# A hybrid sequence layer on one core: gates computed in three parts, decay rows stored from GpSimd's queue, and first-phase stores issued by the engine that made the data

## The chip, the cores and the metric

The kernel runs on one core of a Trainium2 chip. The metric is the device time of one execution in microseconds; the profile shows what each engine did in one such execution. The engines are TensorE (PE; its weight loads are listed as PEld), VectorE (DVE), ScalarE (ACT), GpSimd (POOL) and SyncE (SP), which here only issues DMAs.

## The reference

One layer for two groups: a prompt of 1024 frames and 32 sample frames that continue running streams, all of width 1024. The input is normalised and modulated by adaLN. One combined projection feeds three head groups: four mLSTM heads (a matrix memory), eight heads of forgetting attention (FoX) and a gated MLP. What they give is joined, goes through one output projection and a layer norm, then through a SwiGLU feed-forward layer and a second layer norm. Keys, values, log-forget rows and the mLSTM's final state are outputs too. The part that the change reorders is the gates: for FoX the running sum of the log-forget values enters each score,

```
Ft = jnp.cumsum(logf, axis=1).transpose(0, 2, 1)
logits = (jnp.einsum('bthd,bshd->bhts', qi, k) * FOX_SCALE
          + Fi[..., None] - Ft[:, :, None, :])
```

and for the mLSTM a running maximum over input gate minus forget sum gives the stabiliser `m`, block by block.

## The kernel before

Every matrix product is made from high and low parts in a reduced fp32 format (three products instead of one: L117 to L119 with weights stationary, L282 to L284 with tokens stationary). Weights come by DMA, ScalarE casts the high part (L105), and VectorE or GpSimd makes the low part (L106).

The first phase (`run`) computes for the 1088 columns of the prompt and the samples: first units of the projection (`fm_first`), the FoX values and the gate columns (`tm_unit` with `evac_v`, which fills the tile `G`), then `gates()`, and then a list of units written out in the string `ORDER`. Its letters: `q0` to `q7` are the heads' query and key projections (`head_unit`: products `head_g` for the first 512 columns, `fm_g` for more), `f0` to `f7` the attention of the first four query tiles of a head (`fox`: scores `fox_s`, probabilities `fox_p`, their transposes `fox_t`, outputs `fox_o`), `k` the mLSTM's queries and keys (`fm_unit` with `evac_mqk`), `s` the mLSTM states, `m0` to `m3` mLSTM blocks, `v` and `o` the mLSTM's values and output gates (`evac_raw`), and `a` one unit of the adaLN projection (`ada`, weights in `ada_late`, products at L179, result copied at L182). After the list come the gated MLP, the second halves of the later heads, the output projection, layer norm 1 and the feed-forward part.

The framework's scheduler turns this into one queue of instructions for each engine, from its own estimate of times; attention and mLSTM are put under a higher priority. Within an engine instructions run in queue order, and a wait at the head of a queue holds everything behind it. DMAs issued from SP and from ScalarE also wait until the earlier transfer that used the same one of eight completion counters has landed.

`gates()` takes `G`, makes the log-sigmoid on VectorE, sums along frames with matrix products (L484 to L487), joins the sums of the eight blocks (L497), and writes the decay rows: a tile `fr` of 64 x 6 x 128 with the running sums and their negatives in high and low parts and with ones, stored to the DRAM tile `dfs` by two DMAs. The heads read them back with `decay()` into the last four partitions of `q2` and `k2` (tiles `head_q`, `head_k`), and L769, the second of the two products of a score, needs them; L768, the first, does not. Then `gates()` makes the running maxima by seven VectorE steps, a recurrence over nine blocks (L525 and the lines around), with products at L521 and L529, and the column form of the weights for the mLSTM (`col`, transposed at L547). Its last stores are the states `o_m` and `o_ms` and the tiles `dM` and `dd0` in DRAM. Its tiles lie in a pool of their own that is closed at its end.

All stores of the first phase are issued from SP, in one queue with all loads. GpSimd issues DMAs only late in the kernel (`start_dp`, from 927.6 us on).

Of the kernel before, what the change touches and what calls it, by code (L numbers as in the profile page):

```python
# [15 lines left out]
P = 128  # L16
# [4 lines left out]
NS = 32  # L21
# [48 lines left out]
class Kernel:  # L70
# [18 lines left out]

    def store(self, out, in_):  # L90
        self.nc.sync.dma_start(out, in_)

# [207 lines left out]
    def evac_v(self, half):  # L300
        nc = self.nc

        def evac(tt, ps, n):
            nc.vector.tensor_copy(self.G[:n, tt, 8 * half:8 * half + 8], ps[:n, 256:264])
            cols = slice(256 * half, 256 * half + 256)
            if tt == 8:
                nc.vector.tensor_copy(self.vs[:, cols], ps[:n, :256])
                self.store(self.d["o_vs"][:, cols], self.vs[:, cols])
                return
            raw = self.t(self.sm, [P, 256], F32, "traw", 2)  # L310
            nc.scalar.copy(raw, ps[:, :256])
            self.store(self.d["o_v"][tt * P:(tt + 1) * P, cols], raw)
            hl = self.t(self.sm, [P, 4, 2, 64], F32R, "vhl", 2)
            src = ps[:, :256].rearrange("p (h e) -> p h e", h=4)
            nc.vector.tensor_copy(hl[:, :, 0, :], src)
            nc.vector.tensor_tensor(hl[:, :, 1, :], src, f(hl[:, :, 0, :]), ALU.subtract)
            self.store(self.dv[:, tt, 512 * half:512 * half + 512],
                       f(hl).rearrange("p h two e -> p (h two e)"))
        return evac

    def evac_raw(self, dst):
        nc = self.nc

        def evac(tt, ps, n):
            if tt < 8:
                raw = self.t(self.sm, [P, 256], F32, "traw", 2)
                nc.scalar.copy(raw, ps[:, :256])
                self.store(dst[:, tt, :], raw)
            else:
                self.store(dst[:n, tt, :], ps[:n, :256])  # L330
        return evac
# [27 lines left out]
    def evac_qk(self, h):  # L359
        nc = self.nc  # L360

        def evac(o, n, ps):
# [5 lines left out]
            nc.gpsimd.tensor_tensor(kr[:, :n], f(hi[:, :n]), f(lo[:, :n]), ALU.add)  # L368
            self.store(self.dqh[h, :, o:o + n], f(hi[:, :n]))
            self.store(self.dql[h, :, o:o + n], f(lo[:, :n]))  # L370
            self.store(self.d["o_kT"][h, :, o:o + n], kr[64:, :n])
            if o + n == T:
# [14 lines left out]
    def head_unit(self, h):  # L387
# [17 lines left out]
        for o in (0, 256):  # L405
            kr = self.t(self.sm, [P, 272], F32, "qkr", 2)
            nc.scalar.copy(kr[hi, :256], ps[hi, o:o + 256])
            self.store(self.d["o_kT"][h, :, o:o + 256], kr[hi, :256])
        self.store(self.dqh[h, hi, :512], f(k1[hi]))
        self.store(self.dql[h, hi, :512], f(k2[lo]))  # L410
# [8 lines left out]
    def evac_mqk(self, i, scale):  # L419
        nc = self.nc  # L420

        def evac(o, n, ps):
            r = self.t(self.sm, [P, 272], F32, "qkr", 2)
            nc.scalar.activation(r[:, :n], ps, AF.Copy, scale=scale)
            self.store(self.dmqk[:, i, o:o + n], r[:, :n])
        return evac


    def gates(self):
        self.phase = "gates"  # L430
        nc, d = self.nc, self.d
        ctx = ExitStack()
# [3 lines left out]
        ut = t([64, 64], "ut")  # L436
        nc.gpsimd.memset(ut[:, 0:8], 0.0)
# [3 lines left out]
        rows = self.ident[:R, :R].rearrange("p (j h) -> p j h", h=4)  # L441
        ind, sel, back = t([R, 9], "ind"), t([R, 4], "sel"), t([4, R], "back")
        nc.vector.tensor_reduce(ind, rows, AX.X, ALU.add)
# [3 lines left out]
        pair = lambda x: x.unsqueeze(1).to_broadcast([R, 2, 9])  # L447
        scan = [t([R, 192], "scan0"), t([R, 192], "scan1")]
        for x in scan:
            nc.gpsimd.memset(x[:, 0:64], NEG)  # L450
        fr = t([64, 6, P], "fr", F32R)
        nc.gpsimd.memset(f(fr[:, 2:4, :]), 1.0)
        m0 = t([4, 9], "m0")
        nc.vector.memset(m0[:, 0:1], NEG)
        mm = t([4, 2, 9], "mm")
        self.load(mm[:, 0, 8:9], d["state_m"])

        x = t([P, 9, 16], "gx")
        nc.vector.tensor_tensor(x, self.G, self.rowp[:, 0:16].unsqueeze(1).to_broadcast([P, 9, 16]), ALU.add)
        z = x[:, :, 4:16]  # L460
        a, e, s, s2, p = (t([P, 9, 12], f"g{i}") for i in range(5))
        nc.vector.scalar_tensor_tensor(a, z, -1.0, z, ALU.mult, ALU.min)
# [9 lines left out]
        nc.vector.tensor_scalar(a, z, 0.0, None, ALU.min)  # L472
        ls = t([P, 9, 12], "ls")
# [3 lines left out]
        gi, gm, gn, gf = (t([P, 9, n], f"gw{i}") for i, n in enumerate((4, 4, 4, 8)))  # L477
        nc.vector.tensor_copy(gf, ls[:, :, 4:12])
# [9 lines left out]

        rf = t([72, P], "rf")
        nc.scalar.copy(rf, ps[:72, 256:384])  # L490
        nc.vector.tensor_copy(scan[0][:, 64:192], ps[:R, 0:128])
        rs = t([R, 4, P], "rs")
        nc.scalar.copy(rs[:, 0, :], ps[:R, 0:128])
        b = t([R, P], "gb")
# [3 lines left out]
        fc = t([64, 1], "fc")  # L498
        nc.vector.tensor_copy(fc, pc[:64, 0:1])
        ft = t([64, P], "ft")  # L500
        nc.vector.tensor_scalar(ft, rf[:64], fc, None, ALU.add)
        nc.scalar.copy(fr[:, 4, :], ft)
        nc.vector.tensor_tensor(fr[:, 5, :], ft, f(fr[:, 4, :]), ALU.subtract)
        nc.vector.tensor_scalar(fr[:, 0:2, :], f(fr[:, 4:6, :]), -1.0, None, ALU.mult)
        for r in (slice(0, 32), slice(32, 64)):
            self.store(self.dfs[r], f(fr[r]))
        nc.vector.tensor_copy(self.sf[64:72, :], rf[64:72, 0:NS])

        for i in range(7):
# [3 lines left out]
        A = scan[1][:, 64:]  # L513
        E = t([R, 2], "E")
# [4 lines left out]
        EI = t([R, 2, 9], "EI")  # L519
        nc.vector.tensor_tensor(EI, E.unsqueeze(2).to_broadcast([R, 2, 9]), pair(ind), ALU.mult)  # L520
        nc.tensor.matmul(pc[:4, 32:50], sel, EI.rearrange("p a j -> p (a j)"), start=True, stop=True)  # L521
        ab = t([4, 2, 9], "ab")
        nc.vector.tensor_copy(ab, pc[:4, 32:50].rearrange("p (a j) -> p a j", a=2))
# [5 lines left out]
        nc.tensor.matmul(pc[:R, 64:82], back, mm.rearrange("p a j -> p (a j)"), start=True, stop=True)  # L529
        mt, mc = t([R, 2, 9], "mt"), t([R, 2], "mc")  # L530
        nc.vector.tensor_tensor(mt, pc[:R, 64:82].rearrange("p (a j) -> p a j", a=2), pair(ind), ALU.mult)
        nc.vector.tensor_reduce(mc, mt, AX.X, ALU.add)
        M = t([R, P], "M")
# [4 lines left out]
        self.store(self.dM, M)  # L538
        self.store(d["o_m"], m0[:, 8:9])
        mes, d0 = t([4, 1], "mes"), t([4, 9], "d0")  # L540
        nc.vector.tensor_tensor(mes, mm[:, 1, 8:9], ab[:, 1, 8:9], ALU.add)
        self.store(d["o_ms"], mes)
        nc.vector.tensor_tensor(d0, mm[:, 0, :], mm[:, 1, :], ALU.subtract)
        self.store(self.dd0, d0)
        ps = self.t(self.pt, [P, 512], F32, "t")
# [3 lines left out]
        nc.scalar.activation(self.col[:, :, 1:4, :], self.col[:, :, 1:4, :], AF.Exp)  # L549
        ctx.close()  # L550

# [128 lines left out]
    def to_mix(self, x, j, L, k0, pool, bank=None):  # L680
# [8 lines left out]
        o = j * P - GO[c]  # L689
        self.store(self.dmix[c][:, k0:k0 + 2, o:o + L], s[:, :, :L])  # L690


    def evac_gmlp(self, tt, ps, n, bank=None):
# [28 lines left out]
        w = n * nt  # L722
        self.store(self.dmix[c][:, 6:8, o:o + w], s.rearrange("p i t q -> p i (t q)")[:, :, :w])

# [577 lines left out]
    def run(self):  # L1302
# [343 lines left out]
```

## Time and profile before

| | |
|---|---|
| median of 3 runs | 1389.02 us (1388.13 to 1390.63) |
| profiled execution | 1390.74 us, span 1389.0 us |
| TensorE busy | 1341.3 us, 97% |
| VectorE busy | 1013.7 us, 73% |
| ScalarE busy | 653.7 us, 47% |
| GpSimd busy | 236.2 us, 17% |
| mean granted TensorE clock | 0.988 |

Busy times are sums over one execution. An engine at 97% leaves 48 us of idle time in the whole span, so single waits of one to three microseconds matter, and they are read one by one from TensorE's timeline. The granted clock is a share of full speed: at 0.50 a product takes twice as long.

### The profile page before, as it was taken

The numbers are of one execution on the slowest core, as the hardware profiler recorded it, in microseconds if no ns is written. First come the engines' busy times: TensorE is split into PE (matmuls) and PEld (weight loads), VectorE is DVE, ScalarE is ACT, GpSimd is POOL, SyncE is SP. The second block draws the span as 40 slices with busy tenths as digits, with TensorE's granted clock in tenths as the row PEclk, the third lists the DMA queues.
The fourth block names the chain that finished last, engine by engine and source line by source line (L and its number), as shares of the span: only waits on it lengthen the run. The fifth ranks groups of instructions, "written<-read, shape, count | busy, mean of one in ns | idle before, by whom it ended". The sixth has DMA issues, their size and how long they took to land.

```text
span 1389.0 us, 25227 instructions
## 1 busy us (share of the span) xinstructions
PE 1341.3 (97%) x9432; PEld 1224.2 (88%) x9432; DVE 1013.7 (73%) x2144; ACT 653.7 (47%) x1274; POOL 236.2 (17%) x269
## 2 busy tenths in 40 slices
PE   7997999999999899999999999999999999999996
PEld 4896899988899778888887889899999999999996
DVE  5546643678779757777776766677998988888777
ACT  3313444553545544545544445345574554545355
POOL 1000100032156600000000000264610000000341
PEclk9999899999999999999999999999999999999998
DMA  9764664455765665444443442564597768463321
GB/s 360 252 225 122 187 186 129 128 170 157 224 202 159 171 199 182 125 131 137 135 134 86 107 127 80 187 171 133 160 239 188 214 165 212 139 175 112 102 91 65
DMA packets 123513, 224.65 MB, mean 162 GB/s; under 512 B 21260, under 2 KB 66232, under 8 KB 123392
## 3 DMA queue, kind: packets, MB, share of 16 engines
q1 hardware_dynamic: 118080, 212.95, 49.4%
q0 software_dynamic: 5168, 9.96, 4.6%
q8 instruction: 74, 1.21, 0.4%
q14 instruction: 47, 0.39, 0.1%
q10 hardware_dynamic: 144, 0.14, 0.0%
HBM read 191.21 MB, written 51.72 MB: 175 GB/s over the span
## 4 chain that ended last, share of the span: by engine, by line
PE 83%; DVE 7%; DMA 4%; ACT 2%; issue 2%; SPq 1%; POOL 1%; DVEq 0%; ACTq 0%; POOLq 0%
PE up_g L117 5%; PE up_g L118 5%; PE up_g L119 5%; PE dn_g L119 4%; PE dn_g L117 4%; PE dn_g L118 4%; PE sup_u L119 3%; PE sup_u L117 3%; PE sup_u L118 3%; PE tm_g L283 3%; PE tm_g L282 2%; PE tm_g L284 2%; PE wo_g L119 2%; PE wo_g L117 2%; PE wo_g L118 2%; PE fox_t L804 2%
## 5 line engine op out<-in xcount | busy, mean ns | idle before, releaser
L117 PE MATMUL up_g<-mlstm_ah,up_whi 128*128 128x512 f32 (+1 forms) x384 | 142.2, 371 | 5.1 <-ACT lna_tmp L1053 3.3
L118 PE MATMUL up_g<-mlstm_al,up_whi 128*128 128x512 f32 (+1 forms) x384 | 142.2, 370 | 0.4 <-DVE mlstm_al L1058 0.4
L119 PE MATMUL up_g<-mlstm_ah,up_wlo 128*128 128x512 f32 (+1 forms) x384 | 141.3, 368 | 0.0
L283 PE MATMUL tm_g<-tm_wlo,start_h1h 128*128 128x256 f32 (+1 forms) x384 | 109.4, 286 | 0.9 <-DVE tm_wlo L106 0.9
L282 PE MATMUL tm_g<-tm_whi,start_h1h 128*128 128x256 f32 (+1 forms) x384 | 109.1, 286 | 0.3 <-DVE tm_traw L352 0.2
L284 PE MATMUL tm_g<-tm_whi,start_h1l 128*128 128x256 f32 (+1 forms) x384 | 109.1, 285 | 0.0
L1177 ACT CAST sup_whi<-sup_raw 128x1024 fp32r<-128x1024 f32 x54 | 56.0, 1048 | 91.0 <-PE dn_u L118 47.6
L117 PEld LDWEIGHTS up_g<-mlstm_ah,up_whi 128*128 128x128 f32 x384 | 73.6, 192 | 17.5 <-ACT mlstm_ah L1057 3.5
L118 PEld LDWEIGHTS up_g<-mlstm_al,up_whi 128*128 128x128 f32 x384 | 73.7, 192 | 11.9 <-DVE mlstm_al L1058 1.1
L119 PEld LDWEIGHTS up_g<-mlstm_ah,up_wlo 128*128 128x128 f32 x384 | 73.8, 192 | 10.8
L777 ACT ACTIVATE fox_p<-fox_s,fox_fmx 128x384 f32<-128x384 f32 (+2 forms) x96 | 55.2, 579 | 57.2 <-DVE fox_fmx L775 43.6
L105 ACT CAST up_whi<-up_raw 128x1024 fp32r<-128x1024 f32 x50 | 52.4, 1048 | 61.6 <-PE dn_g L118 20.9
L1032 DVE SCALAR_TENSOR_TENSOR wo_z<-dn_g,start_mod,wo_z 128x512 f32<-128x512 f32 (+4 forms) x120 | 60.2, 519 | 22.5 <-PE dn_g L119 22.0
L1178 DVE TENSOR_TENSOR sup_wlo<-sup_raw,sup_whi 128x1024 fp32r<-128x1024 f32 x54 | 68.1, 1264 | 10.8 <-ACT sup_whi L1177 10.8
L106 DVE TENSOR_TENSOR up_wlo<-up_raw,up_whi 128x1024 fp32r<-128x1024 f32 x50 | 66.8, 1336 | 12.3 <-ACT up_whi L105 11.6
L283 PEld LDWEIGHTS tm_g<-tm_wlo,start_h1h 128*128 128x128 f32 x384 | 72.2, 188 | 2.6 <-issue 1.2
L282 PEld LDWEIGHTS tm_g<-tm_whi,start_h1h 128*128 128x128 f32 x384 | 72.1, 189 | 1.8 <-DVE tm_traw L352 0.7
L117 PE MATMUL dn_g<-up_acth,dn_whi 128*128 128x512 f32 (+2 forms) x200 | 73.5, 368 | 0.0
L118 PE MATMUL dn_g<-up_actl,dn_whi 128*128 128x512 f32 (+2 forms) x200 | 73.3, 368 | 0.0
L119 PE MATMUL dn_g<-up_acth,dn_wlo 128*128 128x512 f32 (+2 forms) x200 | 73.3, 366 | 0.0
L284 PEld LDWEIGHTS tm_g<-tm_whi,start_h1l 128*128 128x128 f32 x384 | 72.2, 188 | 0.5 <-issue 0.4
L105 ACT CAST dn_whi<-dn_raw 128x1024 fp32r<-128x1024 f32 (+1 forms) x44 | 42.7, 971 | 51.0 <-PE up_g L118 11.4
(641 smaller groups left out, 4605.5 us busy)
## 6 DMA issues: line engine op xcount, KB each, us to landing
up_raw<-w_gu SPq DMA_DIRECT2D x50, 512.0 KB
dn_raw<-w_dn SPq DMA_DIRECT2D x28, 512.0 KB
ada_late<-w_ada SPq DMA_DIRECT2D x24, 512.0 KB
wo_raw<-w_o SPq DMA_DIRECT2D x24, 512.0 KB
sup_raw<-w_gu SPq DMA_DIRECT2D x20, 512.0 KB
start_dp<-w_gu SPq DMA_DIRECT2D x19, 512.0 KB
start_dp<-w_gu POOLq DMA_DIRECT2D x19, 512.0 KB, 7.2
sup_raw<-start_dp SPq DMA_DIRECT2D x18, 512.0 KB
```

The lines of the kernel that those rows point to most:

```text
L105: nc.scalar.copy(hi[:, :w], raw[:, :w])
L106: (eng or nc.vector).tensor_tensor(lo[:, :w], raw[:, :w], f(hi[:, :w]), ALU.subtract)
L117: nc.tensor.matmul(ps, hi, xh(k), start=start and k == 0, stop=False)
L118: nc.tensor.matmul(ps, hi, xl(k), start=False, stop=False)
L119: nc.tensor.matmul(ps, lo, xh(k), start=False, stop=stop and k == n - 1)
L282: nc.tensor.matmul(ps[:, :ncol], xh, hi, start=k == 0, stop=False)
L283: nc.tensor.matmul(ps[:, :ncol], xh, lo, start=False, stop=False)
L284: nc.tensor.matmul(ps[:, :ncol], xl, hi, start=False, stop=k == 7)
L777: nc.scalar.activation(pr[:, lo:hi], banks[x][:, :hi - lo], AF.Exp, bias=mxs[:, 0:1], accum_out=sums[:, x:x + 1])
L1032: self.lastz = self.nc.vector.scalar_tensor_tensor(z[:, m, x:y], ps[:, x - a:y - a], g[i], z[:, m, x:y], ALU.mult, ALU.add)
L1177: nc.scalar.copy(h, x)
L1178: tt(l, x, f(h), ALU.subtract)
```

## The change

Three things change, all in the first phase.

`gates()` becomes a generator with two `yield`s. Part 1 (up to the stores of the decay rows) runs where the function stood; part 2 (maxima, recurrence, columns) runs at the first `g` in `ORDER`, part 3 (its other stores) at the second. Since its tiles live longer, they take buffers of the pool of the attention and the mLSTM, which is opened earlier; the tile `fr` is cut into `fk` (rows for keys) and `fq` (rows for queries), and `dfs` is written by four stores instead of two, from GpSimd's queue.

`store` takes an engine. ScalarE now issues the stores of what it copied: 16 of `o_v`, 24 of `dqh`, 16 of `o_kT` in `head_unit`, 8 each of `dmqk`, `dmv` and `dmo`, and 14 of `dmix`: 94 in all. GpSimd issues the 16 of `o_kT` in `evac_qk`, and the four of the decay rows. SP's queue goes from 750 to 638 rows.

```diff
-ORDER = "q0 f0 q1 a f1 a q2 f2 k0 k1p s a q3 f3 a v q4 f4 a q5 f5 o a m0 q6 f6 a m1 q7 m2 f7 a m3"
+ORDER = "q0 f0 g q1 a f1 a g q2 f2 k0 k1p s a q3 f3 a v q4 f4 a q5 f5 o a m0 q6 f6 a m1 q7 m2 f7 a m3"
...
-    def store(self, out, in_):
-        self.nc.sync.dma_start(out, in_)
+    def store(self, out, in_, eng=None):
+        (eng or self.nc.sync).dma_start(out, in_)
...
+            self.store(self.d["o_v"][tt * P:(tt + 1) * P, cols], raw, nc.scalar)
...
+                self.store(dst[:, tt, :], raw, nc.scalar)
...
+            self.store(self.dqh[h, :, o:o + n], f(hi[:, :n]), nc.scalar)
             self.store(self.dql[h, :, o:o + n], f(lo[:, :n]))
+            self.store(self.d["o_kT"][h, :, o:o + n], kr[64:, :n], nc.gpsimd)
...
             nc.scalar.copy(kr[hi, :256], ps[hi, o:o + 256])
+            self.store(self.d["o_kT"][h, :, o:o + 256], kr[hi, :256], nc.scalar)
+        self.store(self.dqh[h, hi, :512], f(k1[hi]), nc.scalar)
...
+            self.store(self.dmqk[:, i, o:o + n], r[:, :n], nc.scalar)
...
-        gp = self.pool("gates", ctx=ctx, side="right")
-        t = lambda shape, tag, dt=F32: self.t(gp, shape, dt, tag)
+        t = lambda shape, tag, dt=F32, bufs=1: self.t(self.mx, shape, dt, tag, bufs)
...
-        fr = t([64, 6, P], "fr", F32R)
-        nc.gpsimd.memset(f(fr[:, 2:4, :]), 1.0)
+        fk = t([64, 4, P], "mqk", F32R)
+        nc.gpsimd.memset(f(fk[:, 2:4, :]), 1.0)
+        fq = t([64, 2, P], "mkw", F32R)
...
-        self.store(d["o_lf"].rearrange("(j p) h -> p j h", p=P), ls[:, 0:8, 4:12])
-        self.store(d["o_lfs"], ls[:NS, 8, 4:12])
...
         for r in (slice(0, 32), slice(32, 64)):
-            self.store(self.dfs[r], f(fr[r]))
+            self.store(self.dfs[r, 4:6], f(fq[r]), nc.gpsimd)
+            self.store(self.dfs[r, 0:4], f(fk[r]), nc.gpsimd)
         nc.vector.tensor_copy(self.sf[64:72, :], rf[64:72, 0:NS])
+        yield
...
+        yield
+        self.store(d["o_lf"].rearrange("(j p) h -> p j h", p=P), ls[:, 0:8, 4:12])
+        self.store(d["o_lfs"], ls[:NS, 8, 4:12])
+        self.store(self.dM, M)
+        self.store(d["o_m"], m0[:, 8:9])
+        self.store(d["o_ms"], mes)
+        self.store(self.dd0, d0)
...
+        self.store(self.dmix[c][:, k0:k0 + 2, o:o + L], s[:, :, :L], nc.scalar)
...
+        self.store(self.dmix[c][:, 6:8, o:o + w], s.rearrange("p i t q -> p i (t q)")[:, :, :w], nc.scalar)
...
-        more(T1[2])
-        self.gates()
-        more(T1[3])
         s2 = ExitStack()
         self.mx = self.pool("mx0", ctx=s2)
+        more(T1[2])
+        gates = self.gates()
+        next(gates)
+        more(T1[3])
...
+            if x[0] == "g":
+                next(gates, None)
+                return ()
```

The scheduler orders all engines anew. The pieces below are queues as the scheduler left them; a number at a name's end tells two tiles of one kind apart, and the brackets name what the instruction waits for (an engine, or a DMA counter). First TensorE before, at the end of the gates: the last of the products `fm_g` of head 1, the gates' two products, the adaLN units and the transposes of `rs`.

```order
L119 MATMUL fm_g_1711<-start_h1h_171,fox_wlo_1661 128x272
L521 MATMUL gates_t_1342<-gates_EI_1366,gates_sel_1280 4x18 [waits DVE_49]
L529 MATMUL gates_t_1342<-gates_mm_1293,gates_back_1281 36x18 [waits DMAHW1_49,DVE_49]
L179 MATMUL ada_t_1407<-ada_late_1408,start_c_63_182 32x256 [waits DMAHW7_49,DVE_49]
L179 MATMUL ada_t_1407<-ada_late_1408,start_c_63_182 32x256 x3
L179 MATMUL ada_t_1407<-ada_late_1414,start_c_63_182 32x256 [waits DMAHW0_49]
L179 MATMUL ada_t_1407<-ada_late_1414,start_c_63_182 32x256 x3
L547 MATMUL gates_t_1399<-start_ident_121,gates_rs_1338 128x36 [waits DVE_49] x2
L547 MATMUL gates_t_1399<-start_ident_121,gates_rs_1338 128x36
L185 MATMUL ada_t_1407<-start_ident_121,ada_adas_1420 128x128 [waits Activation_49]
L185 MATMUL ada_t_1407<-start_ident_121,ada_adas_1420 128x128
L179 MATMUL ada_t_1429<-ada_late_1430,start_c_63_182 32x256 [waits DMAHW4_49,DVE_49]
```

The same engine after, at the first adaLN unit behind the gates' part 1, among the products `fm_g` of head 1.

```order
L119 MATMUL fm_g_1681<-start_h1h_171,gates_wlo_1631 128x272
L117 MATMUL fm_g_1715<-start_h1h_171,gates_whi_1630 128x272 [waits DVE_49]
L118 MATMUL fm_g_1715<-start_h1l_172,gates_whi_1630 128x272
L179 MATMUL ada_t_1339<-ada_late_1340,start_c_63_182 32x256 [waits DMAHW1_49,Activation_49]
L179 MATMUL ada_t_1339<-ada_late_1340,start_c_63_182 32x256 x3
L179 MATMUL ada_t_1339<-ada_late_1346,start_c_63_182 32x256 [waits DMAHW2_49]
L179 MATMUL ada_t_1339<-ada_late_1346,start_c_63_182 32x256 x3
L119 MATMUL fm_g_1715<-start_h1h_171,gates_wlo_1631 128x272
```

The gates' products L521 and L529 (now L534 and the line of the same product after it) no longer stand here; they come some 160 rows later, and the adaLN units stand between products of the heads.

SP before, with the gates' stores, the adaLN weights and the loads of the decay rows (`head_q`, `head_k`).

```order
L91 DMA start_dfs_64<-gates_fr_1289 32x768 [waits DVE_49,DMAHW6_49,Activation_49,Pool_49]
L91 DMA start_dfs_64<-gates_fr_1289 32x768 [waits DMAHW7_49]
L91 DMA o_m<-gates_m_217_1291 4x1 [waits DMAHW0_49,DVE_49]
L91 DMA o_ms<-gates_mes_1393 4x1 [waits DMAHW1_49,DVE_49]
L91 DMA start_dd_11_67<-gates_d_244_1394 4x9 [waits DMAHW2_49,DVE_49]
L91 DMA start_dM_66<-gates_M_1386 36x128 [waits DMAHW3_49,DVE_49]
L87 DMA ada_late_1430<-w_ada 128x1024 [waits DMAHW4_49,PE_49]
L87 DMA fm_d0c_2283<-start_dd_11_67 64x2x9 [waits DMAHW5_49,DMAHW2_49]
L87 DMA ada_late_1436<-w_ada 128x1024 [waits DMAHW6_49,PE_49]
L87 DMA head_q_262_1463<-start_dfs_64 4x4x128 [waits DMAHW7_49]
```

SP after, around the loads of the decay rows; the counters DMASW4 and DMASW2 are those of GpSimd's stores.

```order
L87 DMA ada_late_1362<-w_ada 128x1024 [waits DMAHW6_49,PE_49]
L87 DMA ada_late_1368<-w_ada 128x1024 [waits DMAHW7_49,PE_49]
L91 DMA start_dql_58<-fm_qkl_1707 128x272 [waits DMAHW0_49,DVE_49]
L91 DMA start_dql_58<-fm_qkl_1741 128x272 [waits DMAHW2_49,DVE_49]
L87 DMA head_q_239_1392<-start_dfs_64 4x4x128 [waits DMAHW3_49,DMASW4_49,DMASW2_49]
L87 DMA head_k_237_1390<-start_dfs_64 4x4x128 [waits DMAHW4_49]
```

The adaLN weights moved ahead of the decay rows' loads, and the stores of `dfs`, `o_m`, `o_ms`, `dd` and `dM` are gone from between them.

The third place is on TensorE after, where head 0's attention meets head 1's: its first scores (L782 and L783), the transposes of head 0's probabilities (L818), and the first product behind the evacuation of head 2.

```order
L782 MATMUL fox_s_1774<-head_k_284_1634,head_qp_1636 128x128 [waits Activation_49]
L783 MATMUL fox_s_1774<-head_k_285_1635,head_q_287_1637 128x128 [waits DMAHW6_49,DMAHW5_49]
L782 MATMUL fox_s_1785<-head_k_284_1634,head_qp_1636 128x256 [waits Activation_49]
L783 MATMUL fox_s_1785<-head_k_285_1635,head_q_287_1637 128x256
L818 MATMUL fox_t_1550<-start_ident_121,fox_p_1529 128x128 [waits DVE_49]
L818 MATMUL fox_t_1560<-start_ident_121,fox_p_1529 128x128
L818 MATMUL fox_t_1550<-start_ident_121,fox_p_1540 128x128 [waits DVE_49]
L818 MATMUL fox_t_1560<-start_ident_121,fox_p_1540 128x128
L117 MATMUL fm_g_2077<-start_h1h_171,fm_whi_2017 128x272 [waits Activation_49]
```

Between these nine rows stands no other product, and the one behind them waits for ScalarE's last copy of head 2; before, the same transposes and scores of heads 0 and 1 had `fm_g` products among and behind them that waited for nothing.

More of the change, by code (lines that the diff above doesn't have):

```diff
@@ L431, in gates, with small @@
         nc, d = self.nc, self.d
-        ctx = ExitStack()
-        gp = self.pool("gates", ctx=ctx, side="right")
-        t = lambda shape, tag, dt=F32: self.t(gp, shape, dt, tag)
+        t = lambda shape, tag, dt=F32, bufs=1: self.t(self.mx, shape, dt, tag, bufs)
+        few = t([64, 256], "mo")
+        at = [0]
+        def small(p, *dims):
+            n = 1
+            for x in dims:
+                n *= x
+            y = few[:p, at[0]:at[0] + n]
+            at[0] += n
+            return y.rearrange("p (a b) -> p a b", a=dims[0]) if len(dims) > 1 else y
         R = 36
-        ut = t([64, 64], "ut")
+        ut = small(64, 64)
         nc.gpsimd.memset(ut[:, 0:8], 0.0)
@@ L441, in gates @@
         rows = self.ident[:R, :R].rearrange("p (j h) -> p j h", h=4)
-        ind, sel, back = t([R, 9], "ind"), t([R, 4], "sel"), t([4, R], "back")
+        ind, sel, back = small(R, 9), small(R, 4), small(4, R)
         nc.vector.tensor_reduce(ind, rows, AX.X, ALU.add)
@@ L537, in gates @@
         nc.vector.tensor_scalar(rs[:, 3, :], rs[:, 0, :], mc[:, 1:2], None, ALU.subtract)
-        self.store(self.dM, M)
-        self.store(d["o_m"], m0[:, 8:9])
-        mes, d0 = t([4, 1], "mes"), t([4, 9], "d0")
+        mes, d0 = small(4, 1), small(4, 9)
         nc.vector.tensor_tensor(mes, mm[:, 1, 8:9], ab[:, 1, 8:9], ALU.add)
-        self.store(d["o_ms"], mes)
         nc.vector.tensor_tensor(d0, mm[:, 0, :], mm[:, 1, :], ALU.subtract)
-        self.store(self.dd0, d0)
         ps = self.t(self.pt, [P, 512], F32, "t")
```

57 lines of the change are left out of this document (25 added, 32 removed).

## The prediction

> **What bounds the kernel now.** I read the page first, for the engine that is nearest to its limit, for TensorE's clock, and for the chain of work that ended last.
>
> ```profile
> PE 1341.3 (97%) x9432; PEld 1224.2 (88%) x9432; DVE 1013.7 (73%) x2144; ACT 653.7 (47%) x1274; POOL 236.2 (17%) x269
> PEclk9999899999999999999999999999999999999998
> PE 83%; DVE 7%; DMA 4%; ACT 2%; issue 2%; SPq 1%; POOL 1%; DVEq 0%; ACTq 0%; POOLq 0%
> ```
>
> TensorE is busy for 97% of the span and carries 83% of the chain. So an edit is worth what it takes from TensorE's idle time, plus what it takes from the time at a lower clock. The clock row has one low digit, the fifth of 40 slices (each 34.7 us), and that is where the gates lie. The table by windows splits this place and two later stages (columns: window, length, busy time of PE, PEld, DVE, ACT and POOL with instruction counts, granted clock, DMA share, GB/s).
>
> ```profile
> 125.00:130.00 5.00, 2.90 (x21) 2.27 (x19) 2.87 (x15) 0.30 (x1) 0.00 (x0) 1.00 0.17 39
> 130.00:135.00 5.00, 2.25 (x23) 1.09 (x23) 4.13 (x18) 2.57 (x6) 0.64 (x2) 0.77 0.42 105
> 135.00:140.00 5.00, 1.31 (x12) 0.43 (x16) 1.47 (x3) 3.10 (x7) 0.00 (x0) 0.50 0.72 210
> 140.00:146.00 6.00, 6.00 (x31) 5.22 (x24) 2.93 (x9) 2.07 (x7) 1.71 (x3) 0.50 0.54 142
> 147.00:306.00 159.00, 157.81 (x1175) 142.77 (x1173) 88.48 (x224) 78.57 (x181) 14.68 (x15) 1.00 0.54 161
> 390.00:485.00 95.00, 88.44 (x696) 86.03 (x695) 78.98 (x132) 48.70 (x91) 60.97 (x65) 0.96 0.58 169
> ```
>
> Of the 15 us from 125 to 140 TensorE works 2.90 + 2.25 + 1.31 = 6.46 and is idle for 8.54. From 135 to 146 its clock is granted at 0.50. The heads and the attention that follow (147 to 306) leave only 1.2 us idle. TensorE's timeline shows what it waited for (start, duration, engine, line, operation, then idle time before and its releaser).
>
> ```profile
> 117.04 0.39 PE L117 MATMUL head_g<-start_h1h,fox_whi 128*128 128x512 f32 x1
> ...
> 118.44 0.39 PE L117 MATMUL head_g<-start_h1h,fox_whi 128*128 128x512 f32 x1
> ...
> 126.34 0.29 PE L119 MATMUL fm_g<-start_h1h,fox_wlo 128*128 128x272 f32 x1
> ...
> 127.47 0.29 PE L119 MATMUL fm_g<-start_h1h,fox_wlo 128*128 128x272 f32 x1
> 127.69 0.20 PE L521 MATMUL gates_t<-gates_EI,gates_sel 36*4 36x18 f32 x2
> 130.36 0.24 PE L529 MATMUL gates_t<-gates_mm,gates_back 4*36 4x18 f32 x2 [2.47 <-DVE gates_mm L528]
> ...
> 135.86 1.08 PE L179 MATMUL ada_t<-ada_late,start_c 128*32 128x256 f32 x8 [2.99 <-DVE start_mod L197]
> 139.77 1.08 PE L179 MATMUL ada_t<-ada_late,start_c 128*32 128x256 f32 x8 [2.83 <-DMA ada_late<-w_ada]
> ...
> 142.03 0.43 PE L118 MATMUL fm_g<-start_h1l,fox_whi 128*128 128x272 f32 x1
> ...
> 146.11 0.41 PE L118 MATMUL fm_g<-start_h1l,fox_whi 128*128 128x272 f32 x1
> ```
>
> Three stalls stand in a row behind the gates: 2.47 for VectorE's recurrence, 2.99 for the adaLN evacuation, 2.83 for adaLN weights. That last one starts in SP's queue, as its timeline shows.
>
> ```profile
> 127.14 0.78 SPq L91 DMA_DIRECT2D start_dfs<-gates_fr  x2
> ...
> 131.96 0.36 SPq L87 DMA_DIRECT2D ada_late<-w_ada  x1
> ...
> 133.72 0.32 SPq L87 DMA_DIRECT2D head_q<-start_dfs  x1
> ```
>
> The weights' load goes out at 131.96, behind the gates' stores, which VectorE releases late. The load of the decay rows goes out at 133.72, although those rows were stored at 127.14.
>
> **Part 1, the gates in three parts.** The same instructions are issued, in another order. In the new order TensorE never meets the gates with nothing else queued: between L507 and L534 there are the fm products of the first heads, the next heads, and head 0's scores, and the recurrence on VectorE has that time. SP issues the two adaLN loads before the decay rows' loads, and the small stores of part 3 (o_m, o_ms, dM, dd0) some 17 rows later, so neither keeps them back. So the three stalls go: 8.5 us. What hides the recurrence's 2.5 us is the work of q1 and q2; if it ran out, 2.5 us would come back.
>
> With the idle time the low clock should go. From 142.03 to 146.11 eighteen products take 0.227 each; from 126.34 to 127.47 nine take 0.126. So 140.8 to 146.3 held 2.75 us of work and took 5.5, and the two adaLN groups of 1.08 at 135.86 and 139.77 lost 0.54 each. Together 3.8 us. What is late next is the decay rows (part 2) and the scores of head 1 (part 3). **Sum of part 1: −12.3.**
>
> **Part 2, decay rows through GpSimd's queue.** No small store from GpSimd is in this trace; the nearest rows are its 512 KB issues, a ScalarE issue, and SP's last store, which ends with the span.
>
> ```profile
> L1129 POOL DMA_DIRECT2D start_dp<-w_gu x19: 1026/1035/1522, 927.6 to 1228.2; - x19
> ...
> DMA to landing us min/median/max: 5.9/7.2/11.7
> ...
> L1284 SPq DMA_DIRECT2D o_yT<-wo_z x17: 344/394/402, 1095.7 to 1386.3; - x17
> L1284 ACTq DMA_DIRECT2D o_yT<-wo_z x1: 372/372/372, 1385.7 to 1385.7; - x1
> ```
>
> GpSimd needs 1.035 us for an issue where SP needs 0.78 for both old stores. SP's last store goes out at 1386.3 and the span ends at 1389.0, so a small store lands in at most 2.7 us. When are the rows needed? By the number of products ahead of it, the new order's first score row (L782 of head 0) stands where this trace has 117.04; from there to the first product with decay rows (L783) stand 48 of width 512 at 0.233 ((118.44 − 117.04)/6), 51 of 256 to 272 at 0.126, two adaLN groups at 1.08, and about 1 us of small ones: 11.2 + 6.4 + 2.2 + 1.0 = 20.8, so 137.8. When do they come? The rows were ready at 127.1; the new order puts L507, on which they hang, after 25 more products, so I take 128.0. Four issues end at 132.1, the last lands by 134.8; SP then issues two loads of 0.3, and they land by 138.1. The two times are 0.3 us apart, which is within what I can resolve. Behind the four issues stands one low part of weights on GpSimd (L106), which TensorE meets some 125 rows after L783, more than 10 us later: hidden. **I take +0.5**, with bounds of 0 (landing in 2) and 5.5 (issues of 1.52 and a landing in 5.9, as the 512 KB ones: 2.0 + 3.2 more, beside the 0.3).
>
> The Trainium skill ("SBUF — State Buffer", section "SBUF: two separate sides") speaks against this part: a DMA issued from GpSimd has its descriptors written by GpSimd, and VectorE in a two-port mode locks it out of that. This trace shows a spread of 1026 to 1522 ns and nothing worse, beside a busy VectorE; by the page the part could cost the second rival below.
>
> **Part 3, stores issued by ScalarE.** SP loses 112 rows; ScalarE gains 94, each about 0.37, and GpSimd 16 (the key rows of the later heads) beside the four above. Where does ScalarE's issue delay TensorE? First at one new place, where head 1's first scores, the last transposes of head 0's probabilities and the products behind head 2's evacuation follow each other with nothing between. ScalarE's queue there is: the exponential on which head 1's second score waits, the store of head 2's `dqh`, then four copies of head 2, the last of which frees the bank that TensorE's next products need.
>
> ```profile
> L407 ACT COPY head_qkr<-head_g 64x256 f32<-64x256 f32 x14 | 4.6, 368 | 2.1 <-DMA o_kT<-fm_qkr 1.9
> ...
> L404 ACT ACTIVATE head_q<-head_g 64x512 fp32r<-64x512 f32 x6 | 3.6, 592 | 0.1
> L403 ACT CAST head_k<-head_g 64x512 fp32r<-64x512 f32 x6 | 3.5, 584 | 2.6 <-DVE head_k L402 2.3
> ...
> L91 SPq DMA_DIRECT2D start_dqh<-head_k x8: 452/470/883, 135.3 to 292.4; - x8
> ```
>
> 0.470 + 0.584 + 0.592 + 2 × 0.368 = 2.4, of which TensorE fills some 0.6 with two scores and four transposes (about 0.1 each): **+1.8**, bounded by 0 (ScalarE runs ahead) and 4 (a landing of about 1.9 is waited for as well, as in the first row). A stall of that size can lower the clock:
>
> ```profile
> 375.20 0.59 PE L117 MATMUL fm_g<-start_h1h,fm_whi 128*128 128x272 f32 x1 [2.31 <-ACT tm_gms L719]
> ...
> 378.32 0.37 PE L118 MATMUL fm_g<-start_h1l,fm_whi 128*128 128x272 f32 x1
> ```
>
> After 2.31 us of waiting here, fourteen products took 3.1 us where 1.8 would do: 1.4 lost. I take half of it, **+0.7**. The Trainium skill ("TensorE: Matmul & The Clock Gate", section "Part 1: The HAM clock gate") lets the clock fall after an idle window of about 3.4 us; by that the 0.7 would be 0. The row above disagrees, and I go by the row.
>
> Elsewhere, from 147 to 485, TensorE's waits on ScalarE's copies and on what it now stores are these:
>
> ```profile
> PE fm_g L117 <- ACT tm_gms L719: 2.3, 1, 2.3
> ...
> PE mlstm_s L606 <- DMA mlstm_mqk<-start_dmqk: 1.2, 1, 1.2
> PE fm_g L117 <- ACT head_qkr L407: 1.1, 1, 1.1
> ...
> PE wo_g L117 <- ACT tm_gms L719: 0.9, 1, 0.9
> ```
>
> Each can be one store later: 4 × 0.37 = **+1.5** (bounds −1.2, if the wait for dmqk goes because SP has less queued, and +3, if each is two stores later). Behind a ScalarE store stand its own next copies, and VectorE's low halves wait for those; they have 80 of 159 us free on ScalarE from 147 to 306.
>
> The first layer norm (390 to 485) has GpSimd busy for 61 of 95 us. There 8 of the 16 key stores join it, 8 × 1.035 = 8.3 us ahead of its layer-norm work; on the other side SP gives up 16 issues, and ScalarE's waits on landings get shorter. I take **0 ± 3**. From 485 on the programs are alike.
>
> **Sum:** −12.3 + 0.5 + 1.8 + 0.7 + 1.5 + 0 = −7.8. The profiled execution took 1390.74 (span 1389.0 and 1.74 around it), so 1382.9; the median of the three runs, 1389.02, lies 1.72 under it: **1381.2**. Without the part-3 charges and with 3 us gained in the layer norm it would be −15.3, so 1373.7; with the upper bounds of part 3 and of the layer norm all at once, −12.3 + 0.5 + 4 + 1.4 + 3 + 3 = −0.4, so 1388.6. Neither comes all at once; its own range is 1375 to 1387.
>
> **Rivals.** *The stall moves.* The decay rows come late through GpSimd's queue, and L783 waits 5.5 instead of 0.5, and about 1.4 more goes to the clock: −7.8 + 5.0 + 1.4 = −1.4, so 1387.6. For it: the two times above are 0.3 apart, and 1522 ns and 5.9 us are rows of this kernel. Against it: those carry 512 KB, these at most 64. The page on SBUF, cited above, gives this case a mechanism. Chance 0.10.
>
> *ScalarE as issuer delays the heads (slower).* A head's evacuation is a chain of ScalarE and VectorE, and its two key copies and three ScalarE stores now share one queue. A store can hold ScalarE until an earlier transfer has landed; ScalarE waits so already for buffers:
>
> ```profile
> 145.70 0.37 ACT L407 COPY head_qkr<-head_g 64x256 f32<-64x256 f32 x1 [1.53 <-DMA o_kT<-fm_qkr]
> ...
> 462.41 0.49 ACT L366 ACTIVATE fm_qkh<-fm_g,start_qsc 128x272 fp32r<-128x272 f32 x1 [2.94 <-DMA start_dqh<-fm_qkh]
> ```
>
> Three issues (1.1) and one such wait (2.2 on average) are 3.3 us a head. If TensorE sees half of it, the eight heads cost 13.2: −7.8 + 13.2 = +5.4, so 1394.4. It decides from 7.8 / 8 = 1.0 us a head. Against it stands that TensorE idles only 1.2 us of 159 there, and the next heads' products fill in. Chance 0.15.
>
> *No gain kept.* GpSimd's 8.3 us in the layer norm all reach TensorE, which waits on that stage's results: −7.8 + 8.3 = +0.5, so 1389.5. Against it: SP is relieved there. Chance 0.05.
>
> **Numbers.** The forecast has 0.70. A measurement of this kernel can tell about 0.2%, 2.8 us, from no change, so "same" is 1386.2 to 1391.8: the first and third rivals fall in it, less a little. Faster 0.70, same 0.13, slower 0.17. The range leaves out the slower rival and the forecast's outer edge: 1375.0 to 1391.5.
>
> **What would show it.** Right: the clock at 1.00 from 125 to 146; no wait of TensorE at the gates' lines or on ada_late; L783 of head 0 at about 138 with a wait under 1 us; a wait of about 2 us near head 1's first scores; the first layer norm some 9 us earlier. Wrong: a wait of L783 on the decay rows' loads of several us; waits on head_qkr, fm_qkh or head_k repeated for every head; more idle time from 390 to 485 than the 6.6 us of before.

## The result and the profile after

| | before | changed |
|---|---|---|
| median of 20 runs | 1388.76 us (1384.02 to 1393.89) | 1388.63 us (1386.31 to 1392.60) |
| ratio to before | | 1.0001, 95% interval 0.9990 to 1.0011 |
| profiled execution | 1390.74 us, span 1389.0 | 1387.05 us, span 1384.7 |

No change in time, where 7.8 us less was forecast. The profiled execution of before is 2.0 us above its median and that of the changed kernel 1.6 below its own, so the 3.7 us between the two profiles are chance; what the traces are good for is the place of the waits. At the gates the changed kernel did what was forecast. Its page and its table by windows (columns as before) show it:

```profile
PE 1340.5 (97%) x9432; PEld 1223.4 (88%) x9432; DVE 1019.6 (74%) x2144; ACT 654.5 (47%) x1274; POOL 249.0 (18%) x288
PEclk9999999999999899999999999999999999999998
```

```profile
125.00:130.00 5.00, 5.00 (x48) 4.11 (x47) 2.86 (x15) 1.49 (x4) 1.98 (x4) 1.00 0.36 75
130.00:135.00 5.00, 5.00 (x27) 4.03 (x26) 3.34 (x6) 1.43 (x2) 2.39 (x1) 1.00 0.88 269
135.00:140.00 5.00, 5.00 (x40) 3.47 (x40) 1.79 (x6) 3.71 (x9) 0.00 (x0) 1.00 0.51 137
140.00:146.00 6.00, 5.84 (x48) 5.61 (x46) 5.09 (x16) 2.37 (x7) 2.80 (x5) 1.00 0.95 330
147.00:306.00 159.00, 154.98 (x1143) 137.17 (x1142) 92.25 (x250) 75.86 (x178) 14.76 (x15) 0.99 0.49 148
390.00:485.00 95.00, 86.80 (x648) 82.65 (x647) 80.83 (x137) 50.37 (x97) 58.32 (x68) 0.95 0.59 173
```

From 125 to 140 TensorE is busy for 15.00 of 15 us instead of 6.46, and the clock is at 1.00 throughout. But 147 to 306 now leaves 4.0 us idle instead of 1.2, and 390 to 485 leaves 8.2 instead of 6.6. The clock row has its low digit (the 14th slice) at the first layer norm. What TensorE waited for (line, releaser; total, times, longest):

```profile
PE up_g L117 <- ACT lna_tmp L1067: 5.7, 1, 5.7
PE wo_g L117 <- ACT up_ah L1005: 3.1, 1, 3.1
PE ada_t L185 <- ACT ada_adas L182: 3.1, 3, 2.4
PE fox_s L782 <- ACT fox_p L791: 2.8, 2, 2.0
PE fm_g L117 <- ACT tm_gms L733: 2.6, 1, 2.6
...
PE wo_g L117 <- ACT wo_qs L932: 1.8, 1, 1.8
```

Before, the products of the layer norm had waited like this:

```profile
PE up_g L117 <- ACT lna_tmp L1053: 3.3, 1, 3.3
...
PE up_g L117 <- DVE fm_qkl L367: 1.4, 1, 1.4
```

The second of these waits, some 9 us ahead of the first, is 0.3 in the changed kernel, while the first grew to 5.7. The waits on up_ah (near 900), on ada_adas (2.4 of it near 304) and on wo_qs (near 392) are new. None of these three is at a place for which the sum had a term.

### The profile page after: what moved, and what is told of

It reads as the page before. It is cut to its first block, busy times and chain, and to the rows that moved or that the text cites. A ratio compares the mean times of both kernels' runs of the same rounds, so it can differ in the third digit from the quotient of the medians.

```text
span 1384.7 us, 25170 instructions
## 1 busy us (share of the span) xinstructions
PE 1340.5 (97%) x9432; PEld 1223.4 (88%) x9432; DVE 1019.6 (74%) x2144; ACT 654.5 (47%) x1274; POOL 249.0 (18%) x288
## 4 chain that ended last, share of the span: by engine, by line
PE 84%; DVE 6%; DMA 5%; ACT 2%; issue 1%; SPq 1%; POOL 0%; ACTq 0%; DVEq 0%; POOLq 0%
PE up_g L118 6%; PE up_g L119 6%; PE up_g L117 5%; PE dn_g L117 4%; PE dn_g L119 4%; PE dn_g L118 4%; PE tm_g L283 3%; PE tm_g L282 3%; PE tm_g L284 3%; PE sup_u L119 3%; PE sup_u L117 3%; PE sup_u L118 3%; PE fox_t L818 2%; PE wo_g L117 2%; PE wo_g L118 2%; PE wo_g L119 2%
## 5 line engine op out<-in xcount | busy, mean ns | idle before, releaser
L823 ACT CAST fox_pth<-fox_t 128x512 fp32r<-128x512 f32 (+1 forms) x80 | 41.0, 545 | 62.7 <-PE fox_t L818 62.6
```

## Which part costs, the gates or the stores

Each of the three groups of experiments was measured beside the kernel before, run anew, with medians of 1388.64, 1388.34 and 1388.51 us; a difference to before is that of the medians within a group. The ratios come from the same runs and can differ from it by a few tenths of a us.

**The four corners.** Two edits, alone. In the first, every store goes out from SP again:

```diff
-        (eng or self.nc.sync).dma_start(out, in_)
+        self.nc.sync.dma_start(out, in_)
```

> The gates in three parts as in the changed kernel, but every store from SP, the four stores of the decay rows too. TensorE's order is that of the changed kernel around the gates and that of the kernel before from about its 1340th row on. Theory A (the stores give the gates' 12 us back): the stall and the low clock at 125 to 146 are gone and nothing takes their place, 8 to 12 us faster than before. Theory B (what comes after the gates absorbs the gain, whoever issues the stores): TensorE is some 12 us earlier at 147, but waits more at the later stages, above all for the first layer norm; within 4 us of before.

Measured: 1380.98 us, ratio 0.9945 (0.9931 to 0.9960); in its trace TensorE is busy for all of 125 to 140, at a clock of 1.00. In the second, the kernel before gets the changed `store` calls and keeps its `gates()`, with the decay rows stored from SP:

> The gates as before, in one piece and with the decay rows stored from SP; all other stores issued by the engine that made the data, as in the changed kernel. Theory A: 8 to 12 us slower than before, with new waits of TensorE between 147 and 485 and half clock behind them. Theory B: within 3 us of before, the stall at the gates (8.5 us) still there.

Measured: 1394.40 us, ratio 1.0043 (1.0029 to 1.0056). The gates are worth −7.7 us and the stores cost 5.8. Both are outside theory B's ranges, so B falls; both are also short of theory A's 8 to 12, so A has the direction right and the size too large. Then the changed kernel with one engine's stores back on SP, ScalarE's first:

```diff
-        (eng or self.nc.sync).dma_start(out, in_)
+        (eng if eng is self.nc.gpsimd else self.nc.sync).dma_start(out, in_)
```

> The changed kernel with ScalarE's 94 stores back on SP; GpSimd keeps its 16 key stores and the four of the decay rows. Theory A, with ScalarE's queue as the cost: 6 us or more faster than the changed kernel, no wait of TensorE for a copy of the adaLN evacuation near 304. Theory B: within 3 us of the changed kernel.

Measured: 1384.85 us, ratio 0.9971 (0.9960 to 0.9981), 3.8 us under before and between the two theories' figures. And GpSimd's (the same line with `nc.scalar` for `nc.gpsimd`):

> The changed kernel with GpSimd's 20 stores (keys of the later heads, decay rows) back on SP; ScalarE keeps its 94. If GpSimd's queue in the first layer norm is the cost, TensorE's wait of 5.7 us for lna_tmp falls to about 3.3 and the kernel is 2 to 3 us faster than the changed one. Theory B: that wait stays near 5.7, and the time within 2 us.

Measured: 1382.59 us, ratio 0.9956 (0.9940 to 0.9971), 6 us under before; the layer norm's wait fell as expected, but the time fell by 6 against the changed kernel where 2 to 3 were expected. Putting back either set gains. The waits sort by set. First the kernel without ScalarE's stores, then the one without GpSimd's:

```profile
PE up_g L117 <- ACT lna_tmp L1067: 4.1, 1, 4.1
PE wo_g L117 <- ACT up_ah L1005: 3.0, 1, 3.0
```

```profile
PE up_g L117 <- ACT lna_tmp L1067: 3.3, 1, 3.3
PE ada_t L185 <- ACT ada_adas L182: 2.6, 2, 2.4
```

The wait near 900 belongs to GpSimd's stores, that of 2.4 on ada_adas to ScalarE's. Yet near neither is there a busy issuer. Near 304 ScalarE had been idle for 4.82 us, for VectorE's mlstm_mw, and the adaLN copy, for which TensorE waited, stood behind the exponential that needs it (timelines of ScalarE and of TensorE, the changed kernel):

```profile
302.89 0.63 ACT L617 ACTIVATE mlstm_mw<-mlstm_mw 128x512 f32<-128x512 f32 x1 [4.82 <-DVE mlstm_mw L615]
303.43 0.35 ACT L182 COPY ada_adas<-ada_t 128x256 f32<-128x256 f32 x1
```

```profile
303.83 0.44 PE L185 MATMUL ada_t<-start_ident,ada_adas 128*128 128x128 f32 x2 [2.42 <-ACT ada_adas L182]
```

Near 900 ScalarE waited for loads of `wo_tmp`, which SP issued late and between others, over 400 us after GpSimd's last key store (timelines of ScalarE and of SP):

```profile
900.42 1.59 ACT L1005 CAST up_ah<-wo_tmp 128x272 fp32r<-128x272 f32 x4 [2.19 <-DMA wo_tmp<-start_dmix]
```

```profile
892.36 1.85 SPq L87 DMA_DIRECT2D wo_z<-xT  x4
894.26 0.43 SPq L87 DMA_DIRECT2D sup_w<-w_gu  x1
894.78 1.86 SPq L87 DMA_DIRECT2D wo_tmp<-start_dmix  x4
896.96 2.39 SPq L87 DMA_DIRECT2D wo_raw<-w_o  x2
```

Both waits hang on where something stands in a queue. That suggested a second theory: the cost is not the issuing, but the order into which the scheduler puts everything when one store's engine is another.

**Which of GpSimd's stores.** The changed kernel with the 8 key stores of heads 4 to 7 on SP, and with only the decay rows on SP. First the key stores (`PRE` is 4 in this kernel):

```diff
-            self.store(self.d["o_kT"][h, :, o:o + n], kr[64:, :n], nc.gpsimd)
+            self.store(self.d["o_kT"][h, :, o:o + n], kr[64:, :n], nc.gpsimd if h < PRE else None)
```

> The changed kernel with 8 of GpSimd's 20 stores back on SP: the key rows of heads 4 to 7, which fall beside the first layer norm. ScalarE keeps 94 stores, GpSimd 12 with the decay rows. Theory L (these 8 carry GpSimd's whole cost): like the kernel with all 20 back on SP, 6 us faster than before; TensorE's wait for lna_tmp 3.4 instead of 5.7 and no wait of 3 us on wo_g near 900. Theory D (the decay rows or the early keys carry it): within 2 us of the changed kernel.

Measured: 1384.84 us, ratio 0.9968 (0.9955 to 0.9980): 3.5 us under before (4.4 by the ratio) where all 20 stores gave 6.0 (6.1 by the ratio), so less than theory L expected, and both waits as theory L has them (lna_tmp 3.4, nothing near 900). Then the decay rows:

```diff
-            self.store(self.dfs[r, 4:6], f(fq[r]), nc.gpsimd)
-            self.store(self.dfs[r, 0:4], f(fk[r]), nc.gpsimd)
+            self.store(self.dfs[r, 4:6], f(fq[r]))
+            self.store(self.dfs[r, 0:4], f(fk[r]))
```

> The changed kernel with only the four stores of the decay rows back on SP. Theory L: within 2 us of the changed kernel, the waits of 5.7 at the layer norm and 3 near 900 still there. Theory D, with the decay rows as the cost: 4 us or more faster than the changed kernel.

Measured: 1389.81 us, ratio 1.0005 (0.9996 to 1.0015). The decay rows cost nothing that can be told; theory D falls. The 8 late stores alone on top of the gates:

> The gates in three parts, all stores from SP but the 8 key stores of heads 4 to 7, which GpSimd issues. TensorE's order is that of the kernel with gates alone up to row 3132. Theory L: 3 to 5 us slower than the gates alone (1381.0 there), so about 1385, with the waits at the layer norm (over 4) and near 900 (about 3). Theory D: within 1.5 us of the gates alone.

Measured: 1383.11 us, ratio 0.9955 (0.9941 to 0.9969). That is 2.1 us over the gates alone, less than the 3 to 5 expected, and the intervals overlap: by itself inconclusive. The waits came as expected (lna_tmp 4.2, up_ah 2.7).

## Order or issuing

The scheduler's queues can be compared row by row without running them. TensorE's row order turned out to hang on single stores. The next kernels use that: they differ in one or a few stores and have, on TensorE, either exactly the same order or another.

**ScalarE's side.** The kernel above with the 8 late key stores on SP, now with the 8 dqh stores of `head_unit` on SP as well:

```diff
-        self.store(self.dqh[h, hi, :512], f(k1[hi]), nc.scalar)
+        self.store(self.dqh[h, hi, :512], f(k1[hi]))
```

> As the kernel with the 8 late key stores on SP, and the 8 dqh stores of head_unit on SP too, so that ScalarE issues 86. In its order the adaLN copy no longer stands right behind the mLSTM exponential that ends late near 304. If the wait of 2.4 us there comes of the order, it is gone with 86 stores still on ScalarE, and the time falls by 1 to 3 us against the 94; if it comes of ScalarE's issue time, it stays at 2 or more.

Measured: 1379.23 us, ratio 0.9933 (0.9922 to 0.9945), 5.6 us less than with the 94, more than expected. Its timeline of TensorE has at that place

```profile
303.12 0.44 PE L628 MATMUL mlstm_t<-start_ident,mlstm_mqk 128*128 128x128 f32 x2 [0.78 <-DVE fox_ptl L824]
```

0.78 us instead of 2.42, and the wait of 1.8 on wo_qs near 392 is gone too, with 86 stores still issued by ScalarE. Of the 8 stores only head 7's matters for TensorE's order. So the test was to put back two stores of 114:

```diff
-            self.store(self.d["o_kT"][h, :, o:o + n], kr[64:, :n], nc.gpsimd)
+            self.store(self.d["o_kT"][h, :, o:o + n], kr[64:, :n], nc.gpsimd if h < 7 or o == 512 else None)
...
-        self.store(self.dqh[h, hi, :512], f(k1[hi]), nc.scalar)
+        self.store(self.dqh[h, hi, :512], f(k1[hi]), nc.scalar if h < 7 else None)
```

> The changed kernel with 2 of its 114 moved stores back on SP: head 7's second key store (from GpSimd) and head 7's dqh store of head_unit (from ScalarE). TensorE's order is then, row by row, that of the kernel with 86 ScalarE stores and 12 of GpSimd (1379.2). Theory P (the scheduler's other order costs, not the issuing): 1378 to 1381, 8 to 10 us faster than the changed kernel, with the waits near 304, of 5.7 at the layer norm and near 900 gone. Theory I (issuing and contention cost): two of 114 stores change the time by less than 1 us, so 1388.

Measured: 1381.31 us, ratio 0.9951 (0.9934 to 0.9967): 7 us faster than the changed kernel for two stores, where theory P expected 8 to 10, and 0.3 above the range that it gave. Theory I falls. With 112 stores still issued by ScalarE and GpSimd, the kernel is as fast as with the gates alone and every store from SP (1380.98; TensorE's order is another there up to about 490 us), so no cost of issuing can be told from these times. Theory P missed one thing: the wait for lna_tmp did not go.

```profile
PE up_g L117 <- ACT lna_tmp L1067: 5.2, 1, 5.2
```

With the first of the two edits alone:

> The changed kernel with one store back on SP, head 7's second key store. TensorE's and ScalarE's orders are those of the kernel with 8 key stores back (1384.8). Theory P: 1383 to 1386; the wait near 304 stays, that near 900 is gone. Theory I: within 1 us of the changed kernel.

Measured: 1384.47 us, ratio 0.9973 (0.9962 to 0.9985), the same as with all 8 late stores back; lna_tmp 5.7, ada_adas 2.4, nothing near 900. One store's engine is worth 4 us, and its interval does not touch the changed kernel's (0.9990 to 1.0011).

**GpSimd's side.** The gates alone, with the 6 key stores of heads 4 to 6 on GpSimd:

```diff
+            (nc.gpsimd if h in (4, 5, 6) else nc.sync).dma_start(self.d["o_kT"][h, :, o:o + n], kr[64:, :n])
```

> The gates in three parts, all stores from SP but the 6 key stores of heads 4 to 6, which GpSimd issues. TensorE's order is, row by row, that of the kernel with the gates alone. Theory P: within 1.5 us of the gates alone (1381.0), no wait near 900. Theory I: six eighths of what the eight stores cost, 1.2 us or more slower, and the wait for lna_tmp over 4.

Measured: 1378.25 us, ratio 0.9927 (0.9913 to 0.9942), the fastest of all. It is 2.7 us under the gates alone, outside theory P's 1.5 on the good side, though the two intervals overlap; theory I's slowdown is not there, but its wait for lna_tmp is (4.2). And with head 7's second key store only:

```diff
+            (nc.gpsimd if h == 7 and o > 512 else nc.sync).dma_start(self.d["o_kT"][h, :, o:o + n], kr[64:, :n])
```

> The gates in three parts, all stores from SP but one, head 7's second key store, which GpSimd issues. TensorE's order is, row by row, that of the kernel with 8 late key stores on GpSimd (1383.1), other than that of the gates alone from row 3132 to 5432. Theory P: as slow as with the eight, 1.5 to 4 us over the gates alone, with a wait of 2 to 3 us on wo_g near 897. Theory I: like the gates alone.

Measured: 1382.42 us, ratio 0.9960 (0.9944 to 0.9975). That is 1.4 us over the gates alone, just under theory P's range, and those two intervals overlap: beside the gates alone this run decides nothing. Beside the kernel with six stores it does, for the two intervals do not touch: one store in the one order takes 4.2 us more than six in the other. The waits of the kernel with one store:

```profile
PE up_g L117 <- ACT lna_tmp L1067: 3.4, 1, 3.4
PE wo_g L117 <- ACT up_ah L1005: 3.0, 1, 3.0
```

The two waits have different causes. The one near 900 (2.4 to 3.1 us) is there in the six kernels that share TensorE's order in that part and in none of the others, whether GpSimd issues one late store or eight. The order shows in when SP issues the loads. With one store put back (the kernel of 1384.47) SP issues the first of the four `wo_tmp` loads concerned at 892.72, and TensorE comes to the first product of that stage (`wo_g`) at 899.26:

```profile
892.72 0.37 SPq L87 DMA_DIRECT2D wo_tmp<-start_dmix  x1
```

```profile
899.26 0.29 PE L117 MATMUL wo_g<-up_ah,wo_whi 128*128 128x272 f32 x1
```

In the changed kernel the same loads go out from 894.78, and TensorE came to that product at 894.63.

The wait for lna_tmp grows to between 4.1 and 5.9 wherever six or more late stores are GpSimd's, whatever the order. Part of this is a wait that moved: beside the gates alone, the wait for lna_tmp goes from 3.4 to 4.2 with six such stores, and a wait of 0.8 for fm_qkl ahead of it goes. No cost of the wait can be told from the times. There are four pairs of kernels with the same TensorE order, one with six to eight of the late stores on GpSimd and one with none or one. The first of each pair is 2.7 us faster (1378.25 against 1380.98), 0.4 faster (1384.47 against 1384.84), 0.7 slower (1383.11 against 1382.42) and 2.1 slower (1381.31 against 1379.23; there seven dqh stores of ScalarE differ too), and in each pair the intervals overlap.

## Why the prediction was wrong, step by step

**Part 1 was right.** The stall at the gates and the low clock went, as the windows show. The gates alone gave −7.7 us by the median (−10.3 with six stores moved), so not all of the 12.3 arrives at the end. The 3.8 us for the clock were too much: the sum took a product at 0.50 to last twice as long, and by its own rows it is 0.227 against 0.126 us, 1.8 times, which makes it 3.4. In the traces of before and of the gates alone, TensorE is 10.6 us ahead at 226 (times of before), still 10.5 at 495, and 9.1 at 521: between the last two a new wait of 0.9 for ada_adas stands. Why 10.6 and not 12 arrives at 226 was not settled.

**Part 2 was right, for a partly wrong reason.** GpSimd's queue and TensorE's timeline:

```profile
127.36 1.00 POOL L91 DMA_DIRECT2D start_dfs<-gates_mkw  x2 [5.65 <-DVE gates_mo L530]
128.35 0.99 POOL L91 DMA_DIRECT2D start_dfs<-gates_mqk  x2
```

```profile
138.54 0.39 PE L783 MATMUL fox_s<-head_k,head_q 68*128 68x128 f32 x2
```

An issue takes 0.50 us, half of the 1.035 taken from the 512 KB rows. L783 ran at 138.54 (137.8 forecast) without a wait; the +0.5 was 0. The rival of the stall that moves did not happen (it is the first of the three; the sentence on the Trainium skill calls it the second). The Trainium skill ("SBUF — State Buffer", section "SBUF: two separate sides") has VectorE in a two-port mode hold up a DMA that GpSimd issues; no price of that shows here, for the kernel with the decay rows on SP is no faster.

**Part 3 was right at its place.** Where +1.8 was charged, TensorE waited 0.80 + 0.27 + 0.54 = 1.6:

```profile
146.63 0.38 PE L782 MATMUL fox_s<-head_k,head_qp 128*128 128x256 f32 x1 [0.80 <-ACT fox_p L791]
...
147.41 0.44 PE L818 MATMUL fox_t<-start_ident,fox_p 128*128 128x128 f32 x2 [0.27 <-DVE fox_p L799]
148.38 0.69 PE L818 MATMUL fox_t<-start_ident,fox_p 128*128 128x128 f32 x2 [0.54 <-DVE fox_p L799]
148.84 0.59 PE L117 MATMUL fm_g<-start_h1h,fm_whi 128*128 128x272 f32 x1
149.24 0.43 PE L118 MATMUL fm_g<-start_h1l,fm_whi 128*128 128x272 f32 x1
...
151.50 0.34 PE L119 MATMUL fm_g<-start_h1h,fm_wlo 128*128 128x272 f32 x1
```

The products behind it ran at a granted clock of 0.50 (149 to 151). Ten of them, from 149.24 to 151.50, took 0.226 each instead of 0.126, so 1.0 us or more went there, where +0.7 was charged. No single wait in this place was longer than 0.80 us. This again speaks for the row and against the idle window of about 3.4 us in the Trainium skill ("TensorE: Matmul & The Clock Gate", section "Part 1: The HAM clock gate").

**Two terms failed.** "Elsewhere, from 147 to 485 ... +1.5" added a store's issue to four waits that stood in the old order. Of those four only the first grew: 2.3, 1.2, 1.1 and 0.9 became 2.6, 0.7, none and none. But the order was new there, and had waits of its own near 304 (2.4) and 392 (1.8), which went when one ScalarE store of head 7 was put back; that store is worth 3.2 us by the medians (1384.47 to 1381.31), with intervals that just overlap. And "From 485 on the programs are alike" was false: TensorE's rows are the same only from the 5432nd of 9055 on, at about 913 us, and SP's only in its last 155 or so. In the part of SP's queue that differs lie the loads for which TensorE waits 3.1 us near 900, and changing the order back by one store gave 4.2 us (1388.63 to 1384.47). So the gain was given back by the new order in two places, not by the rivals.

The rival on ScalarE had the right sign and the wrong mechanism: a chain in each of eight heads was its place, but the waits are single ones. The third rival (GpSimd in the layer norm) named a real wait, and the sign that went with it came true (8.2 us of idle time from 390 to 485, over 6.6), but no cost of that wait in the time can be told. The layer norm itself came 6 us earlier (TensorE is through at 465.52 instead of 471.67), not 9.

Two agreements are luck. The measured 1388.63 lies within the outer range and between the figures of the first and the third rival (1387.6 and 1389.5), and neither did what it names. The kernel with two stores put back meets the forecast, 1381.31 against 1381.2, but by errors that cancel: the gates gave −7.7 for −12.3, and the stores then cost 0.3 for the +4.5 of parts 2 and 3. The lower edge of the sum, −15.3, also leaves out the 0.5 of part 2; with it, it is −14.8.

## What to carry to other kernels

Where a scheduler orders the queues, an edit to one DMA's engine is an edit to the whole order behind it: compare the orders of before and after to their last differing row, and price each wait in the new order, not the old waits plus a surcharge. When a change of many small moves nets to nothing, put single moves back and pick those that leave the order alone; two stores of 114 carried 7 us here. A profile's own execution was up to 3.5 us off its kernel's median here (1387.94 against 1384.47), so the size of a small effect belongs to the medians and only its place to the trace.

## What the hardware showed that was not expected

GpSimd issued small stores in 0.50 (32 and 64 KB) to 0.55 us (key rows), where its 512 KB ones took 1.03. In the layer norm some of VectorE's sums got slower where GpSimd worked beside them: eight of L1063 took 5.33 us in the changed kernel against 3.98 of the same line (L1049) before, and a step of the chain ahead of them 1.49 instead of 0.42. VectorE's timeline after, then before:

```profile
454.10 1.49 DVE L960 SCALAR_TENSOR_TENSOR lna_tmp<-lna_tmp,wo_pv 128x256 f32<-128x256 f32 x1 [0.32 <-ACT wo_pv L959]
...
457.16 5.33 DVE L1063 TENSOR_TENSOR wo_z<-wo_z,wo_pv 128x256 f32<-128x256 f32 x8
```

```profile
462.21 0.42 DVE L946 SCALAR_TENSOR_TENSOR lna_tmp<-lna_tmp,wo_pv 128x256 f32<-128x256 f32 x1
...
464.66 3.98 DVE L1049 TENSOR_TENSOR wo_z<-wo_z,wo_pv 128x256 f32<-128x256 f32 x8
```

The two differences are 1.07 + 1.35 = 2.4 us, but a step between them got shorter (0.43 instead of 0.88), and the chain from the first of these rows to ScalarE's next step (L1067, before L1053) takes 8.8 us instead of 6.8. The wait for lna_tmp grew by 2.4 (3.3 to 5.7), while the wait ahead of it fell by 1.1 (1.4 to 0.3); how the two hang together was not settled. While VectorE's longest of these sums ran, from 459.10 on for 1.86 us, GpSimd worked without a gap on a copy and two sums between two DMA issues:

```profile
459.04 0.23 POOL L373 COPY start_qks<-fm_qkr 128x32 f32<-128x32 f32 x1
459.21 0.74 POOL L1064 TENSOR_TENSOR wo_z<-wo_z,wo_qs 128x256 f32<-128x256 f32 x1
459.91 0.75 POOL L368 TENSOR_TENSOR fm_qkr<-fm_qkh,fm_qkl 128x272 f32<-128x272 f32 x1
```

Before, two of the eight sums met a sum on GpSimd and took 0.95 and 0.96 us, and the others 0.41 to 0.54. The first of the two (VectorE, then GpSimd):

```profile
465.79 0.95 DVE L1049 TENSOR_TENSOR wo_z<-wo_z,wo_pv 128x256 f32<-128x256 f32 x1
```

```profile
465.61 0.86 POOL L1050 TENSOR_TENSOR wo_z<-wo_z,wo_qs 128x256 f32<-128x256 f32 x1 [0.69 <-DVE wo_z L1049]
```

So it is GpSimd's sums that go with the slow ones, with or without stores in its queue, and in the changed kernel more of them fell there: GpSimd's sum for a key row waited for the landing of an earlier key store (1.54 us before the one at 451.32, 1.22 before the one at 457.35). That the two engines hold each other up is argued from these rows; no run took GpSimd's sums away alone.
